# A hybrid decoder trunk on one core: second projection of the first convolution half in one piece, early products along the second half's taps, no ahead splits in short pairs

## Chip, core and metric

The kernel runs on one core of a Trainium2 chip. A core has five engines with their own in-order queues: TensorE (matrix products, PE in the profile, its weight loads PEld), VectorE (DVE), ScalarE (ACT), GpSimd (POOL) and SyncE (SP), which here issues the DMAs. The metric is the device time of one launch in microseconds (us), as the median of several runs.

## What is computed

Two layers over x of 1024 positions by 1024 channels, float32, batch 1:

```
layer 0: x = x + fox_attention(rms_norm(x));   x = x + conv_ffn(rms_norm(x))
layer 1: x = x + conformer_conv(rms_norm(x));  x = x + conv_ffn(rms_norm(x))

conv_ffn(h):        u = causal_dwconv(h @ w_up, w_dw, 3 taps) + b_dw       # w_up: 1024 x 5632
                    gate, val = split(u);  (silu(gate) * val) @ w_down     # w_down: 2816 x 1024
conformer_conv(h):  a, g = split(h @ w_pw1 + b_pw1);  u = a * sigmoid(g)
                    u = silu(rms_norm(causal_dwconv(u, w_dw, 31 taps) + b_dw))
                    u @ w_pw2 + b_pw2                                      # w_pw2: 1024 x 1024
```

Attention, before all this, is not touched by the change.

## The kernel before

Every matrix operand is held as two halves: `hi` is the value rounded to TensorE's faster 4-byte format (a ScalarE cast), `lo` what is left (a subtraction). A product is three passes, hi x hi, hi x lo and lo x hi (`mm3`, lines 183 to 189), into one PSUM bank of 128x512. A "product" in this document is one such pass of 512 columns. Weights come from DRAM raw; `weight` (line 215) casts on ScalarE and lets POOL subtract (`split`, lines 179 to 181), unless a low half lies in DRAM, which is then only loaded. `split_ahead` (line 227) makes such a low half ahead of time: cast on ScalarE, subtraction on VectorE (line 235), two DMAs. The list `T.ahead` holds 76 of them: 32 blocks of the convolution's first projection (`pwlo`), then 44 blocks of layer 0's `w_down` (`dnlo`, 22 row blocks f by two column halves nh).

The tokens are worked in two halves of 512 (h = 0, 1). An up-projection (`up`, line 327) takes the channels in 22 pairs of 128 gate and 128 value channels and computes each pair for both token halves with seven products of 12 passes instead of eight (a Strassen-like scheme): factors t1 to t4 of the activations are made once on VectorE and ScalarE (`combine`, line 258), sums of weights s1 to s4 on POOL. Two of the seven (p1 and p2) need only the first token half, and `early` (line 302) can compute them in advance and park them in DRAM; a pair whose two are parked is a short pair, with five products. In layer 0 nine pairs are short, in layer 1 all 22. Within the loop over pairs (lines 435 to 443) the products p4 and p3 of a pair come after the next pair's first products, and after each pair some ahead splits are recorded:

```
for step in a + before + b:
    step()
before = c
for _ in range(min(ahead[f >= done], len(self.ahead))):   # ahead = (2, 4): short pair 2, full pair 4
    self.ahead.pop(0)()
```

VectorE adds the parked or fresh results (u3 at line 410, u2 at line 400) and does the three taps (line 374) from PSUM, six banks for all.

The down-projection (`down`, line 239) of a token half runs column half by column half; each of its 22 steps f is 12 products into four banks. Its activations are split on VectorE in the first token half of layer 0 and in layer 1, on POOL in the second token half of layer 0 (`los` given). After the second column half the residual x is complete and a norm follows; with `lag` its transposes on TensorE (`norm_block`, line 118) are put off until some products later (`tick`).

The convolution module (`conv`, line 860) also runs by token half, channel tile by channel tile (8). `glu` computes 48 products and u; `taps_of` does 31 taps: 21 on VectorE (line 913), 10 as ScalarE product and POOL addition (lines 905 to 918), then the sum y and, on POOL, the running sum of squares `sqa` (line 927). The norm needs that sum: a row product `ssps` on TensorE (line 944), a broadcast `rb` (line 954), then VectorE and ScalarE make the halves of y (lines 959 to 962). `rest` is the second projection, 192 products in 16 steps, with the late norms behind it.

What order TensorE works in is written by hand, by generators that are advanced in turns (`turns(a, b, n, m)`: n steps of a, then m of b). The other engines' orders are set by a scheduler that plans ahead on the same program; each engine then runs its own queue strictly in that order. The turns around the change, at the end of `trunk`:

- the first convolution half's taps (`main0`) take turns 5 to 2 with the second token half of layer 0's down-projection (`down1`); three more steps of `down1`, then the norm;
- the second half's taps (`main1`) take turns 3 to 1 with a filler: first the second projection of the first half (`rest0`), then the early products of layer 1's up-projection;
- the rest of these early products runs after the second half's projection, beside `combine`.

## Time and profile before

| | |
|---|---|
| runs | 2424.33 us median of 3 (2422.46 to 2425.63) |
| profiled execution | 2430.27 us, span 2428.5 us from first to last instruction |
| TensorE busy | 2281.0 us (94% of the span), mean granted clock 0.972 |
| VectorE busy | 1654.8 us (68%) |
| ScalarE busy | 1410.9 us (58%) |
| POOL busy | 1480.1 us (61%) |
| DMA | 391.88 MB, mean 161 GB/s |

Attention takes about the first 600 us, its output projection to 675, layer 0's up-projection from about 747 to 1158, its down-projection to about 1480, beside it from 1300 the first convolution half; the second half's taps reach to 1731, layer 1's up-projection goes from 1878 to 2180, the last down-projection to the end. Durations come from one execution, and a busy TensorE is not TensorE at its peak, so the waits of TensorE are read from its own rows: the bracket at the end of a row is the idle time in front of it and what ended that.

### The profile page before, as it was taken

Reading aid. Unit: us, or ns where it says so; the run is one execution under the profiler, and the core shown is the slowest. Engines: PE = TensorE matmul, PEld = TensorE weight load, DVE = VectorE, ACT = ScalarE, POOL = GpSimd, SP = SyncE. Lnnn points to the kernel's source line nnn. Section 1 sums busy time; section 2 is a strip of 40 time slices with the busy share of each in tenths; the row PEclk is TensorE's granted clock in tenths of the full one; section 3 lists DMA queues with packets and bytes.
Section 4 is the critical chain, followed back from the end, with each engine's and each line's share of the span. In section 5 each row is a group of like instructions: output and inputs, shape, how many; then the busy total and the mean of one; then the engine's idle time right before and its main releaser. Section 6 shows DMA issues by size and latency. Waiting matters only on the chain. (4 is left out here: it accounts for less than half of the span.)

```text
span 2428.5 us, 35460 instructions
## 1 busy us (share of the span) xinstructions
PE 2281.0 (94%) x11282; PEld 1948.8 (80%) x11282; DVE 1654.8 (68%) x2801; ACT 1410.9 (58%) x2992; POOL 1480.1 (61%) x1258
## 2 busy tenths in 40 slices
PE   7899999999988799998999998978898999999998
PEld 6899999988866678877887886757687888878887
DVE  6577777776384887777645885697427798885554
ACT  6566666665244666666546666566545566664443
POOL 2355554443067767775546887577658999954443
PEclk9999999999989999999999999988899999999999
DMA  4222222252155655556768786463344444566664
GB/s 129 63 78 78 79 79 75 58 199 99 66 172 176 196 170 184 188 190 233 270 201 262 248 272 199 156 195 109 127 152 160 148 152 152 159 210 201 205 214 152
DMA packets 365692, 391.88 MB, mean 161 GB/s; under 512 B 26392, under 2 KB 244288, under 8 KB 365504
## 3 DMA queue, kind: packets, MB, share of 16 engines
q1 hardware_dynamic: 365504, 389.61, 50.4%
q8 instruction: 89, 1.46, 0.2%
q14 instruction: 99, 0.81, 0.1%
HBM read 298.22 MB, written 82.90 MB: 157 GB/s over the span
## 5 line engine op out<-in xcount | busy, mean ns | idle before, releaser
L181 POOL TENSOR_TENSOR wlo<-raw,whi 128x512 fp32r<-128x512 f32 (+1 forms) x368 | 522.1, 1422 | 373.5 <-ACT whi L180 361.7
L180 ACT CAST whi<-raw 128x512 fp32r<-128x512 f32 (+2 forms) x504 | 306.0, 632 | 298.1 <-PE dn L187 191.9
L186 PE MATMUL c<-bhi,whi 128*128 128x512 f32 x880 | 346.4, 394 | 30.8 <-DVE u L410 26.4
L187 PE MATMUL c<-blo,whi 128*128 128x512 f32 x880 | 345.5, 393 | 0.0
L188 PE MATMUL c<-bhi,wlo 128*128 128x512 f32 x880 | 345.0, 392 | 0.0
L374 DVE SCALAR_TENSOR_TENSOR acc<-c,ffntab,acc 128x511 f32<-128x511 f32 (+1 forms) x352 | 280.4, 805 | 89.1 <-ACT edge L367 61.4
L181 DVE TENSOR_TENSOR wlo<-raw,whi 128x512 fp32r<-128x512 f32 (+1 forms) x136 | 182.1, 1342 | 140.1 <-ACT whi L180 139.9
L186 PE MATMUL dn<-whi,whi 128*128 128x512 f32 x704 | 275.4, 391 | 0.0
L187 PE MATMUL dn<-wlo,whi 128*128 128x512 f32 x704 | 274.5, 390 | 0.0
L188 PE MATMUL dn<-whi,wlo 128*128 128x512 f32 x704 | 274.4, 390 | 0.0
L181 POOL TENSOR_TENSOR wlo<-sum,whi 128x512 fp32r<-128x512 f32 x176 | 250.5, 1430 | 29.1 <-ACT whi L180 23.5
L913 DVE SCALAR_TENSOR_TENSOR cacc<-u,ctaps,cacc 128x512 f32<-128x512 f32 x320 | 238.4, 754 | 9.1
L186 PEld LDWEIGHTS c<-bhi,whi 128*128 128x128 f32 x880 | 166.9, 190 | 70.5 <-DVE u L410 20.0
L918 POOL TENSOR_TENSOR pacc<-pacc,prod 128x512 f32<-128x512 f32 x144 | 186.7, 1297 | 22.7 <-ACT prod L917 15.2
L188 PEld LDWEIGHTS c<-bhi,wlo 128*128 128x128 f32 x880 | 167.0, 190 | 35.0
L187 PEld LDWEIGHTS c<-blo,whi 128*128 128x128 f32 x880 | 166.8, 190 | 34.6
L115 POOL TENSOR_SCALAR ss<-ss 128x4 f32<-128x4 f32 (+1 forms) x96 | 21.6, 225 | 272.4 <-ACT hn L123 122.4
L186 PE MATMUL pj<-whi,hthi 128*128 128x384 f32 (+1 forms) x512 | 180.2, 353 | 6.1 <-ACT sqr L583 3.6
L364 ACT ACTIVATE acc<-c,ffntab 128x512 f32<-128x512 f32 x176 | 136.0, 788 | 85.3 <-DMA c<-c11d 53.9
L187 PE MATMUL pj<-wlo,hthi 128*128 128x384 f32 (+1 forms) x512 | 177.9, 347 | 0.6 <-DVE wlo L181 0.6
L188 PE MATMUL pj<-whi,htlo 128*128 128x384 f32 (+1 forms) x512 | 178.1, 348 | 0.0
L671 POOL TENSOR_SCALAR x<-x,nm 128x896 f32<-128x896 f32 (+7 forms) x128 | 100.9, 793 | 106.1 <-DVE nm L670 76.4
(204 smaller groups left out, 5733.8 us busy)
## 6 DMA issues: line engine op xcount, KB each, us to landing
raw<-in_ffn_w_up_dram SPq DMA_DIRECT2D x238, 256.0 KB
raw<-actd SPq DMA_DIRECT2D x176, 256.0 KB
raw<-in_ffn_w_down_dram SPq DMA_DIRECT2D x176, 256.0 KB
raw<-in_conv_w_pw_dram SPq DMA_DIRECT2D x96, 256.0 KB
actd<-acc SPq DMA_DIRECT2D x88, 256.0 KB
wlo<-pwlo SPq DMA_DIRECT2D x64, 256.0 KB
raw<-in_fox_w_in_dram SPq DMA_DIRECT2D x64, 192.0 KB
xd<-x SPq DMA_DIRECT2D x24, 512.0 KB
```

The costliest lines, as they stand in the source:

```text
L115: nc.gpsimd.tensor_scalar(ss, ss, 1.0 / n, EPS, op0=ALU.mult, op1=ALU.add)
L180: self.nc.scalar.copy(hi, raw)
L181: (self.nc.vector if vector else self.nc.gpsimd).tensor_tensor(lo, raw, f32(hi), op=ALU.subtract)
L186: nc.tensor.matmul(out, lh, rh, start=start, stop=False, skip_group_check=more)
L187: nc.tensor.matmul(out, lh, rl, start=False, stop=False, skip_group_check=more)
L188: nc.tensor.matmul(out, ll, rh, start=False, stop=stop, skip_group_check=more)
L364: nc.scalar.activation(acc, ps, AF.Identity, bias=tap[3], scale=tap[2])
L374: nc.vector.scalar_tensor_tensor(acc[:, j:], ps[:, : 512 - j], tap[2 - j], acc[:, j:], op0=ALU.mult, op1=ALU.add)
L671: nc.gpsimd.tensor_scalar(X[:, :L], X[:, :L], nm[:, 2:3], 1.0, op0=ALU.mult, op1=ALU.mult)
L913: nc.vector.scalar_tensor_tensor(acc, win(j), tap(j), acc, op0=ALU.mult, op1=ALU.add)
L918: nc.gpsimd.tensor_tensor(pacc, pacc, t, op=ALU.add)
```

## The change

Four edits. (1) Ahead splits are recorded only after full pairs, four each; none after short pairs, and what is left in the list at the end is not done: 52 of the 76. A `w_down` block without a low half in DRAM is split when it is used. (2) The second projection of the first convolution half runs in one piece before the second half; the second half's taps take turns with early products alone, four to one, once the late norms are through. (3) At the end of both up-projections the down-projection's first two steps are put between the last pair's p7, p4 and p3; x is fetched three steps later. (4) Five instead of three steps of `down1` stand between the first half's taps and its norm.

```diff
--- before
+++ after
@@ -51,7 +51,7 @@
 
 N_POOL = 10
 CONV_DOWN = (5, 2)
-CONV_FILL = (3, 1)
+CONV_FILL = (4, 1)
 LAG = 36
 LEAD = (8, 11)
 
@@ -242,7 +242,7 @@
         pss = [self.pup.tile([P, 512], F32, tag="up", name=self.n("dn")) for _ in range(4)]
         for j, (get, r) in enumerate(zip(lhs, rows)):
             hi, lo = get()
-            wh, wl = self.weight(r[:, m], [P, 512], los[nh][j] if los else None)
+            wh, wl = self.weight(r[:, m], [P, 512], los.get((nh, j)) if los else None)
             for b in range(4):
                 c = slice(b * P, (b + 1) * P)
                 self.mm3(pss[b], hi[:, c], lo[:, c], wh, wl, j == 0, j == len(lhs) - 1)
@@ -324,8 +324,7 @@
                 done.append(g)
                 yield
 
-    def up(self, l, fac, w_up, tab, actd, done, p1d, c11d, ahead):
-
+    def up(self, l, fac, w_up, tab, actd, done, p1d, c11d):
 
         nc = self.nc
         wu = w_up[l].rearrange("(k p) f -> p k f", p=P)
@@ -436,11 +435,12 @@
             for step in a + before + b:
                 step()
             before = c
-            for _ in range(min(ahead[f >= done], len(self.ahead))):
+            for _ in range(min(4, len(self.ahead)) if f >= done else 0):
                 self.ahead.pop(0)()
             yield
         for step in before:
             step()
+            yield
 
     def down_acts(self, xs, l, h, actd, w_down, after, los=None):
 
...
@@ -1077,7 +1078,7 @@
     def early(l, keep):
         yield from T.early(l, keep["ht0"], w_up, keep["p1d"], keep["c11d"], keep["done"], keep["stop"])
 
-    def ffn_up(l, keep, first):
+    def ffn_up(l, keep, first, then):
 
         with ExitStack() as st:
             T.ap = st.enter_context(tc.tile_pool(name=f"act{l}", bufs=1, reuse_waits="tile"))
@@ -1090,13 +1091,18 @@
             turns(T.combine(fac, keep["ht0"], keep["b12"], keep["b22"]), first, 1, (lead + 3) // 4)
             keep["stop"].append(True)
             steps(first)
-            steps(T.up(l, fac, w_up, tabs[l], actd, len(keep["done"]), keep["p1d"], keep["c11d"], (2, 4)))
-            while T.ahead:
-                T.ahead.pop(0)()
+            up = T.up(l, fac, w_up, tabs[l], actd, len(keep["done"]), keep["p1d"], keep["c11d"])
+            steps(up, NF)
+            steps(then, 1)
+            steps(up, 1)
+            steps(then, 1)
+            steps(up)
 
     def ffn_down(l, h, xd, after, los=None):
-        T.fetch_x(xs, xd, h)
-        yield from T.down_acts(xs, l, h, actd, a["ffn_w_down"], after, los)
+        for i, _ in enumerate(T.down_acts(xs, l, h, actd, a["ffn_w_down"], after, los)):
+            if i == 3:
+                T.fetch_x(xs, xd, h)
+            yield
 
     keep = {"xd": xds[0]}
     T.attn_out(a["x"][0], xs, ot, wo, normer(gains[0], keep))
@@ -1115,7 +1121,7 @@
 
     w_pw1 = a["conv_w_pw1"][0]
     pwlo = [[dram.tile([P, 4, P], F32, name=f"pwlo{i}_{q}") for q in range(2)] for i in range(2 * KT)]
-    dnlo = [[dram.tile([P, 512], F32, name=f"dnlo{nh}_{f}") for f in range(NF)] for nh in range(2)]
+    dnlo = {}
     for ct in range(KT):
         for s in range(2):
             for q in range(2):
@@ -1125,9 +1131,15 @@
     for nh in range(2):
         for f in range(NF):
             src = a["ffn_w_down"][0, f * P : (f + 1) * P, nh * 512 : (nh + 1) * 512]
-            T.ahead.append(lambda src=src, lo=dnlo[nh][f]: T.split_ahead(src, lo))
+
+            def make(src=src, i=(nh, f)):
+                dnlo[i] = dram.tile([P, 512], F32, name=f"dnlo{i[0]}_{i[1]}")
+                T.split_ahead(src, dnlo[i])
+
+            T.ahead.append(make)
     begin(0, keep)
-    ffn_up(0, keep, early(0, keep))
+    down0 = ffn_down(0, 0, xds[0], lambda tb: conv_norm(tb))
+    ffn_up(0, keep, early(0, keep), down0)
     keep1 = {"xd": xds[2]}
     begin(1, keep1)
     with ExitStack() as st:
@@ -1149,33 +1161,32 @@
             return T.conv(xs, xds[1], h, hc[h], w_pw1, pwlo, taps, vec, a["conv_w_pw2"][0], halo,
                           normer(gains[2], keep1, True))
 
-        steps(ffn_down(0, 0, xds[0], conv_norm))
+        steps(down0)
         down1 = ffn_down(0, 1, xds[0], conv_norm, dnlo)
         while T.lagging:
             steps(down1, 1)
         main0, norm0, rest0 = conv(0)
         turns(main0, down1, *CONV_DOWN)
-        steps(down1, 3)
+        steps(down1, 5)
         turns(norm0, down1, 1, 1)
         steps(down1)
+        steps(rest0)
+        main1, norm1, rest1 = conv(1)
+
         while T.lagging:
-            steps(rest0, 1)
-        main1, norm1, rest1 = conv(1)
-
-        def fill():
-            yield from rest0
-            while T.lagging:
-                yield
-            yield from early(1, keep1)
-
-        filler = fill()
+            steps(main1, 1)
+        filler = early(1, keep1)
         turns(main1, filler, *CONV_FILL)
         steps(filler, 4)
         turns(norm1, filler, 1, 1)
         steps(rest1)
-    ffn_up(1, keep1, filler)
-    for h in range(2):
-        steps(ffn_down(1, h, xds[2], lambda tb: nc.sync.dma_start(a["out"][0, tb * P : (tb + 1) * P, :], xs[tb])))
+    downs = [
+        ffn_down(1, h, xds[2], lambda tb: nc.sync.dma_start(a["out"][0, tb * P : (tb + 1) * P, :], xs[tb]))
+        for h in range(2)
+    ]
+    ffn_up(1, keep1, filler, downs[0])
+    for g in downs:
+        steps(g)
 
 
 # ---- launch: one core; inputs and outputs as the reference has them ----
```

In the rows of the programs below a name is a tile and its numbers say which buffer.

POOL at the end of the first convolution half, before: `wlo` is a split, `pacc` the addition of a tap, `sqa` the running sum of squares.

```order
L918 TENSOR_TENSOR pacc_16400<-pacc_16400,prod_16474 128x512
L181 TENSOR_TENSOR wlo_16659<-raw_16656,whi_16658 128x512
L918 TENSOR_TENSOR pacc_16400<-pacc_16400,prod_16479 128x512
L181 TENSOR_TENSOR wlo_16701<-raw_16698,whi_16700 128x512
L918 TENSOR_TENSOR pacc_16400<-pacc_16400,prod_16485 128x512
L181 TENSOR_TENSOR wlo_16733<-raw_16730,whi_16732 128x512
L918 TENSOR_TENSOR pacc_16400<-pacc_16400,prod_16490 128x512
L181 TENSOR_TENSOR wlo_16823<-raw_16820,whi_16822 128x512
L918 TENSOR_TENSOR pacc_16400<-pacc_16400,prod_16495 128x512
L927 TENSOR_TENSOR sqa_14719<-sqa_14719,sq_16499 128x512
```

The same place now, from nine rows ahead of the second last sum:

```order
L181 TENSOR_TENSOR wlo_16539<-raw_16536,whi_16538 128x512
L181 TENSOR_TENSOR wlo_16545<-raw_16542,whi_16544 128x512
L181 TENSOR_TENSOR wlo_16655<-raw_16652,whi_16654 128x512
L181 TENSOR_TENSOR wlo_16673<-raw_16670,whi_16672 128x512
L181 TENSOR_TENSOR wlo_16691<-raw_16688,whi_16690 128x512
L919 TENSOR_TENSOR pacc_16001<-pacc_16001,prod_16219 128x512
L181 TENSOR_TENSOR wlo_16735<-raw_16732,whi_16734 128x512
L181 TENSOR_TENSOR wlo_16779<-raw_16776,whi_16778 128x512
L919 TENSOR_TENSOR pacc_16001<-pacc_16001,prod_16224 128x512
L928 TENSOR_TENSOR sqa_14551<-sqa_14551,sq_16228 128x512
L919 TENSOR_TENSOR pacc_16232<-pacc_16232,prod_16237 128x512
L919 TENSOR_TENSOR pacc_16232<-pacc_16232,prod_16242 128x512
```

Before, splits and additions alternate up to the last sum; now the splits come in runs, and all nine additions of the last channel tile stand behind them. Between the sums of channel tiles 3 and 7 there are 22 splits before and 46 now, with 36 additions in both.

TensorE around the broadcast `rb` of the first half's norm, before; `dn` is a bank of a down-projection or of the second projection:

```order
L187 MATMUL dn_15750<-wlo_16665,whi_16658 128x512
L188 MATMUL dn_15750<-whi_16664,wlo_16659 128x512
L954 MATMUL rb_16631<-dg_16680,ones 128x512
L186 MATMUL dn_15747<-whi_16706,whi_16700 128x512
L187 MATMUL dn_15747<-wlo_16707,whi_16700 128x512
```

And now:

```order
L187 MATMUL dn_15582<-wlo_16545,whi_16538 128x512
L188 MATMUL dn_15582<-whi_16544,wlo_16539 128x512
L955 MATMUL rb_16511<-dg_16560,ones 128x512
L186 MATMUL dn_16648<-whi_16654,hthi_3388_16566 128x512
L187 MATMUL dn_16648<-wlo_16655,hthi_3388_16566 128x512
L188 MATMUL dn_16648<-whi_16654,htlo_3390_16568 128x512
```

The 24 products of the down-projection that followed `rb` now stand ahead of the norm's row product, and the second projection, which reads the new halves of y (`hthi`, `htlo`), follows at once.

TensorE at the end of the first up-projection, before (`c` is a bank of the up-projection; the rows go from p7 to p4 of the last pair):

```order
L186 MATMUL c_2587_13038<-bhi_8839,whi_13156 128x512
L187 MATMUL c_2587_13038<-blo_8840,whi_13156 128x512
L188 MATMUL c_2587_13038<-bhi_8839,wlo_13157 128x512
L186 MATMUL c_2587_13038<-bhi_8843,whi_13200 128x512
L187 MATMUL c_2587_13038<-blo_8844,whi_13200 128x512
L188 MATMUL c_2587_13038<-bhi_8843,wlo_13201 128x512
```

And now:

```order
L186 MATMUL c_2551_12902<-bhi_8795,whi_13020 128x512
L187 MATMUL c_2551_12902<-blo_8796,whi_13020 128x512
L188 MATMUL c_2551_12902<-bhi_8795,wlo_13021 128x512
L186 MATMUL dn_13068<-whi_13080,whi_13074 128x512
L187 MATMUL dn_13068<-wlo_13081,whi_13074 128x512
L188 MATMUL dn_13068<-whi_13080,wlo_13075 128x512
```

Twelve products of the down-projection come between p7 and p4, and twelve more between p4 and p3.

## Rows read from the trace of the kernel before

**Rows 1.** Windows by stage: us, busy (count) of PE, PEld, DVE, ACT, POOL, clock, DMA.
```profile
747.00:890.00 143.00, 121.18 (x509) 96.79 (x508) 100.96 (x126) 76.72 (x159) 104.71 (x76) 0.98 0.57 182
...
1144.00:1168.00 24.00, 17.66 (x68) 14.25 (x68) 19.60 (x29) 16.47 (x37) 6.64 (x5) 0.86 1.04 406
...
1615.00:1660.00 45.00, 21.67 (x85) 16.12 (x83) 33.74 (x65) 27.65 (x64) 29.74 (x27) 0.67 0.29 96
...
1850.00:1880.00 30.00, 21.75 (x85) 17.09 (x85) 16.20 (x14) 13.54 (x27) 25.53 (x19) 0.89 0.60 191
1880.00:2170.00 290.00, 290.00 (x1281) 240.15 (x1280) 247.56 (x308) 185.72 (x391) 266.83 (x184) 1.00 0.50 153
2170.00:2195.00 25.00, 22.39 (x93) 18.04 (x92) 20.52 (x28) 15.41 (x32) 7.55 (x6) 0.93 0.86 305
```

**Rows 2.** Timeline of TensorE: start, length, line, tiles [idle before, releaser].
```profile
812.25 0.50 PE L186 MATMUL c<-bhi,whi 128*128 128x512 f32 x1 [3.04 <-DVE u L410]
...
1150.55 0.77 PE L186 MATMUL c<-bhi,whi 128*128 128x512 f32 x1 [6.34 <-DVE u L410]
...
1488.26 1.01 PE L944 MATMUL ssps<-ones,sqa 128*128 128x1 f32 x4 [6.41 <-POOL sqa L927]
...
1731.30 1.86 PE L944 MATMUL ssps<-ones,sqa 128*128 128x1 f32 x8 [9.55 <-POOL sqa L927]
...
1817.64 1.03 PE L132 MATMUL nps<-ident,hn 128*128 128x128 f32 x8
...
1878.62 0.39 PE L186 MATMUL c<-bhi,whi 128*128 128x512 f32 x1
...
2175.14 0.47 PE L186 MATMUL c<-bhi,whi 128*128 128x512 f32 x1 [2.61 <-DVE u L410]
```

**Rows 3.** Window 753 to 890 of line 235 alone: VectorE busy.
```profile
753.00:890.00 137.00, 15.34 (x14) 0.98 0.55 176
```

**Rows 4.** Timeline of VectorE at the end of the first up-projection.
```profile
1143.56 0.69 DVE L235 TENSOR_TENSOR araw<-araw,ahi 128x512 fp32r<-128x512 f32 x1 [1.13 <-ACT ahi L234]
...
1149.72 0.68 DVE L410 TENSOR_TENSOR u<-c,p 128x512 f32<-128x512 f32 x1
```

**Rows 5.** Window 1396 to 1488 of lines 181, 918, 927: POOL busy.
```profile
1396.43:1488.26 91.83, 0.00 (x0) 28.53 (x22) 0.99 0.80 263
1396.43:1488.26 91.83, 46.65 (x36) 0.99 0.80 263
1396.43:1488.26 91.83, 6.46 (x5) 0.99 0.80 263
```

**Rows 6.** Timeline of VectorE around the first half's norm.
```profile
1485.51 0.69 DVE L921 TENSOR_TENSOR y<-cacc,pacc 128x512 f32<-128x512 f32 x1 [9.25 <-POOL pacc L918]
...
1498.16 5.36 DVE L959 SCALAR_TENSOR_TENSOR y<-y,cvec,rb 128x512 f32<-128x512 f32 x8 [5.54 <-PE rb L954]
1503.44 1.24 DVE L962 TENSOR_TENSOR htlo<-y,hthi 128x512 fp32r<-128x512 f32 x1
...
1514.77 1.11 DVE L158 SCALAR_TENSOR_TENSOR htlo<-nps,gtab,hthi 128x128 fp32r<-128x128 f32 x4
```

**Rows 7.** Line 913 (duration ns min/median/max), and VectorE timeline of u.
```profile
L913 DVE SCALAR_TENSOR_TENSOR cacc<-u,ctaps,cacc x320: 743/756/759, 1317.3 to 1720.8; 128x512 f32<-128x512 f32 x160
...
1547.32 0.75 DVE L891 SCALAR_TENSOR_TENSOR u<-pw,cvec,sg 128x512 f32<-128x512 f32 x1 [11.71 <-ACT sg L888]
...
1617.28 0.75 DVE L891 SCALAR_TENSOR_TENSOR u<-pw,cvec,sg 128x512 f32<-128x512 f32 x1 [0.84 <-ACT sg L888]
...
1682.00 0.75 DVE L891 SCALAR_TENSOR_TENSOR u<-pw,cvec,sg 128x512 f32<-128x512 f32 x1 [3.03 <-ACT sg L888]
...
1703.76 0.75 DVE L891 SCALAR_TENSOR_TENSOR u<-pw,cvec,sg 128x512 f32<-128x512 f32 x1 [4.38 <-ACT sg L888]
```

**Rows 8.** Timeline of VectorE, combining of layer 1: first and last operation.
```profile
1819.33 0.85 DVE L278 TENSOR_TENSOR t<-b,hthi 128x512 f32<-128x512 f32 x1
...
1866.96 3.10 DVE L272 TENSOR_TENSOR blo<-t,bhi 128x512 fp32r<-128x512 f32 x5 [2.67 <-ACT bhi L271]
```

More of the change, by code (lines that the diff above doesn't have):

```diff
@@ L858, in conv_tables, with conv @@
         return taps, vec
-    def conv(self, xs, xd, h, ht, w_pw1, los, taps, vec, w_pw2, halo, after, n_pool=N_POOL):
+    def conv(self, xs, xd, h, ht, w_pw1, los, taps, vec, w_pw2, halo, after):
         nc = self.nc
@@ L865, in conv @@
         H = C - 1
+        n_pool = N_POOL
         sp = self.sp
```

## Prediction, before the changed kernel was timed

> **What bounds the kernel.** I read the engine totals first, then the windows by stage, then TensorE's own rows with the wait in front of each, and last the rows of the engine named as releaser. TensorE is busy 94% of the span. From 1880 to 2170 us it runs 1281 matrix products in 290 us, 0.2264 us each, with nothing lost [rows 1]; I use that as the price of one product of 512 columns. TensorE's program holds the same 11141 instructions before and after, so no work is saved there: the change can only move time that TensorE loses. A stretch's loss is its length less its products at 0.2264 us; this includes what the clock costs after a wait (granted clock 0.67 to 0.98 in the windows with losses, 1.00 in the one without).
>
> The stretches that the change touches lose: the short pairs of the first up-projection (747 to 890), 143 - 509 x 0.2264 = 27.8 us; the end of that up-projection (1144 to 1168), 24 - 68 x 0.2264 = 8.6; the end of the second one (2170 to 2195), 25 - 93 x 0.2264 = 3.9; its start (1850 to 1880), 30 - 85 x 0.2264 = 10.8; and the taps of the second convolution half, where 1615 to 1660 alone has TensorE busy 21.7 of 45 us [rows 1]. The waits themselves are in [rows 2].
>
> **A. Short pairs split no weights ahead: -23 us.** A short pair is 60 products, 13.6 us. In the second up-projection all 22 pairs are short and take just that, without ahead splits. In the first, 509 products are 8.5 pairs of 16.9 us, and in seven of the nine pairs the product that needs VectorE's sum u3 (line 410) waits 2 to 3 us, as at 812.25 [rows 2]. The difference between the two is two ahead splits per pair: 14 subtractions at line 235, 15.3 us of VectorE in 137 us [rows 3]. The change takes them out and moves none into the full pairs, which keep four each; 52 splits remain of 76. So these pairs should run as those of layer 1 do: 27.8 us back, less about 5 for the first two pairs, since the second up-projection also loses at its start (1850 to 1880). Bounds: -27.8, and -8 if the wait has another cause.
>
> **B. End of the first up-projection: -7 us.** TensorE waits 6.34 us at 1150.55 for u3 [rows 2]. VectorE is late since, just ahead of it, it does ahead splits which themselves wait for ScalarE (1143.56, 1.13 us; u3 only at 1149.72) [rows 4]; six of them were flushed after the loop. They are gone, and 12 products (2.7 us) of the down-projection now stand in the gap. They need two more subtractions of activations on VectorE (0.7 us each, by the u3 row) and a PSUM bank that is freed just before u3. Of 8.6 us I take back 7; bounds 2 and 8.6.
>
> **C. End of the second up-projection: -2.5 us.** The same 12 products fill a wait of 2.61 us at 2175.14 [rows 2]; bounds 0 and -3.9.
>
> **D. 24 weight splits return to POOL: +18.7 us.** Of the first down-projection's 44 weight blocks only 20 now have a low half in DRAM. The other 24 are split on POOL in its second token half, that is while POOL also adds the first convolution half's taps. Between the squares' sum of channel tile 3 (1396.43) and the row product that ends the norm's wait (1488.26) POOL does 22 splits in 28.53 us, 36 additions in 46.65, 5 sums in 6.46 [rows 5]: 81.6 of 91.8 us, and TensorE at 1488.26 has already waited 6.41 us for the last of these sums [rows 2]. So POOL ends last here, and VectorE with it (9.25 us idle for POOL at 1485.51) [rows 6]. In the changed order 46 splits stand between the same two sums: 24 x 28.53/22 = 31.1 us more. POOL's idle time can take up to 10.5 of it; I let it take 7, since half of the gaps are waits for ScalarE in an order that remains. That is 24.1 us later; but 24 products (5.4 us) that stood behind the norm's row product now stand before it. +18.7. Bounds: +15 with all idle time used, less 5 if ScalarE paces the splits earlier than I think, and +25.7 with none. The DMAs saved (24 low halves written and read) lie beside it and cost nothing now.
>
> The same subtraction took VectorE 0.69 us on its best rows and takes POOL 1.30 [rows 4, 5]. [...]
>
> **E. The first half's norm without cover: +7 us.** Before, 24 products stood between the broadcast of the norm's scale (rb) and the second projection, which needs VectorE's results. Now the second projection follows rb at once. VectorE needs 5.36 us for eight multiplications and 1.24 for the first low half [rows 6]; two wider multiplications come between in the new order, at 0.67 each by the first of these rows. 7.9 us, less rb and the two products that need no low half. Bounds 0 (if the 24 products still cover) and +10.
>
> **F. Second projection in one piece, products ahead along the taps: -3 us.** (1) The projection's 192 products and the first 48 of the next half now run before the first tile u of the taps: 112 products more than before (25.4 us). The old order lost time here: from 1498.16 to the first u at 1547.32 are 49.2 us for 152 products and 32 transposes, some 38 us [rows 6, 7]. About half of the 11 us goes, since products that need no transposed block now stand behind the transposes: first u about 20 us later. (2) From first u to the norm's row product the old order took 1731.30 - 1547.32 = 184.0 us [rows 2, 7]. Its first four channel tiles took 17.5 us each; then the four late norms of the residual stream came between two tiles' taps, and 1617.28 to 1682.00 took 64.7 us for two. In the new order these norms stand in the first tile: VectorE has 21 taps of 0.756, eight groups of four narrow subtractions (1.11 each) and three wider operations (0.75) ahead of the second u [rows 6, 7], 27 us, and TensorE's next 24 products come after the last transposes, so about 37 us. Then the tiles hold 78 products (17.7 us) against VectorE's 21 taps, u and one sum, 17.3: I take 18.3. From last u to the row product 27.5 as before (1703.76 to 1731.30). 37 + 6 x 18.3 + 27.5 = 174.3: 10 us less. (3) Behind it 96 products (21.7 us) fewer remain, all of them from the stretch that hid the combining of the factors (lines 278 to 287). That takes VectorE from 1819.33 to 1870.1 [rows 8]. The last transposes end at 1818.7 and 120 products behind them at 1846; the 24 products that need only the factors made first find work, the ones behind them start at 1870. Before, the up-projection's first product was at 1878.62 and these 24 later, at 1884 [rows 2]: 14 of the 21.7 us are kept. 20 - 10 - 14 = -4; I take -3 for the clock after the new waits. Bounds: -20 and +18.
>
> Sum: -23 - 7 - 2.5 + 18.7 + 7 - 3 = -9.8 us. The profiled execution took 2430.27 us (span 2428.5), so 2420.5 in its frame; the median of the three runs shown, 2424.33, lies 5.9 lower: 2414 us. About 0.2% (5 us) is what a measurement of this kernel can tell from no change.
>
> **Rivals.** R1, the taps of the second half run free: the late norms cost the first tile only 25 us and the rest runs at 17.5, as 1547 to 1617 did. Then F is 12 + 5 lower: 2397 us. For it speaks that pace; against it, that the eight groups are released one by one through two PSUM banks. Chance 0.20.
>
> R2, the other side: with less filler behind them the tiles of the second half are paced by VectorE, POOL and ScalarE together, at 21.8 us as 1682.00 to 1703.76 [rows 7]. 6 x 3.5 = 21 us more, 2435 us, slower. It decides from about 20.8 us per tile on. Against it: that interval held 96 products (21.7 us) and is TensorE's own pace. Chance 0.13.
>
> R3, the short pairs' wait does not come from the splits but from the length of the chain through VectorE or from the reloaded first products: A gives 8 us and not 23: 2429 us. Against it stands the second up-projection, whose pairs have the same chain. Chance 0.10.
>
> My forecast has 0.57, by itself 2403 to 2425. It is faster by over 0.2% in 0.42 of all, within it in 0.12, slower in 0.03; R1 adds 0.20 to faster, R2 0.13 to slower, R3 0.06 to no change and 0.04 to slower. Together 0.62, 0.18, 0.20. The range 2396 to 2434 reaches to the middle of R1 and of R2.
>
> **What would show it.** A: pairs of 13.6 us in the first up-projection, no waits of 3 us for line 409's sum. B, C: at both ends the 12 products inside the gap and under 2 us of wait. D: TensorE waits 20 to 28 us before the first half's row product, with POOL busy all the time; a wait under 12 us refutes it. E: a wait of 6 to 9 us at the second projection's first low half. F: the late norms within the first tile, about 18 us from u to u after that, and a wait of 10 us or more at the second up-projection's first products. The forecast fails if D is absorbed or if the tiles of the second half take over 20 us.

## The result and the profile after

The changed kernel takes 2431.19 us (median of 19 runs, 2426.28 to 2438.66), the kernel before 2424.33 (19 runs beside them): ratio 1.0028, 95% interval 1.0020 to 1.0036. It is slower by some 7 us, where 10 us faster was forecast. Its profiled execution took 2436.2 us (span 2434.4).

The windows of the changed kernel, columns as in [rows 1]:

```profile
748.00:890.00 142.00, 142.00 (x628) 117.56 (x627) 109.75 (x142) 89.37 (x183) 120.68 (x86) 1.00 0.47 148
1116.00:1135.00 19.00, 14.19 (x57) 11.33 (x55) 14.79 (x20) 10.84 (x23) 5.34 (x4) 0.91 0.96 381
...
1872.00:2177.00 305.00, 298.88 (x1297) 246.21 (x1296) 271.71 (x330) 195.30 (x413) 272.59 (x186) 0.98 0.50 154
```

The short pairs (first line) now run 628 products in 142.0 us, 0.226 us each: no loss at all, against 509 in 143 us in [rows 1]. The end of the first up-projection (second line) loses 19 - 57 x 0.2264 = 6.1 us where it lost 8.6. The second up-projection (last line) loses 305 - 1297 x 0.2264 = 11.4 us, nearly all of it at its start: its first 48 products take 22.1 us, where they took 10.9. TensorE's rows at the places of [rows 2], with the waits that are new:

```profile
1123.66 0.77 PE L186 MATMUL dn<-whi,whi 128*128 128x512 f32 x1 [4.81 <-DVE acc L373]
...
1484.14 1.87 PE L945 MATMUL ssps<-ones,sqa 128*128 128x1 f32 x8 [26.63 <-POOL sqa L928]
...
1499.42 0.80 PE L186 MATMUL dn<-whi,hthi 128*128 128x512 f32 x1 [4.06 <-ACT hthi L962]
...
1503.23 0.79 PE L188 MATMUL dn<-whi,htlo 128*128 128x512 f32 x1 [2.60 <-DVE htlo L963]
...
1574.79 1.11 PE L132 MATMUL nps<-ident,hn 128*128 128x128 f32 x4 [7.90 <-DVE htlo L158]
...
1747.96 1.87 PE L945 MATMUL ssps<-ones,sqa 128*128 128x1 f32 x8 [20.61 <-POOL sqa L928]
...
1878.91 0.79 PE L187 MATMUL c<-blo,whi 128*128 128x512 f32 x1 [2.61 <-DVE blo L272]
...
1887.14 0.50 PE L186 MATMUL c<-bhi,whi 128*128 128x512 f32 x1 [2.13 <-DVE u L399]
...
2182.79 0.76 PE L186 MATMUL dn<-whi,whi 128*128 128x512 f32 x1 [3.36 <-DVE acc L373]
```

The two row products of the convolution's norms wait 26.6 and 20.6 us for POOL's running sum, where they waited 6.4 and 9.6 [rows 2]. All other new waits are under 8 us.

Both traces hold the same number of TensorE instructions (11282; the forecast's 11141 stands on neither page of the profile). So the start of one and the same product in both traces tells how far the changed kernel is ahead or behind there. Two such products, before and after (the second product after is in the rows above):

```profile
1301.10 0.49 PE L186 MATMUL pw<-hthi,whi 128*128 128x512 f32 x1 [0.43 <-ACT hthi L155]
...
1503.45 0.39 PE L186 MATMUL dn<-whi,hthi 128*128 128x512 f32 x1
```

```profile
1271.31 0.51 PE L186 MATMUL pw<-hthi,whi 128*128 128x512 f32 x1 [0.44 <-ACT hthi L155]
```

The table is worked out from such rows; the last column is what happened since the line above.

| product or tile | before | after | shift | since then |
|---|---|---|---|---|
| first `c`, layer 0 | 746.99 | 748.41 | +1.4 | +1.4 |
| first `pw` | 1301.10 | 1271.31 | -29.8 | -31.2 |
| first product of the second projection's first half | 1503.45 | 1499.42 | -4.0 | +25.8 |
| first u of the second half | 1547.32 | 1568.51 | +21.2 | +25.2 |
| second half's row product | 1731.30 | 1747.96 | +16.7 | -4.5 |
| 49th `c`, layer 1 | 1889.50 | 1894.35 | +4.9 | -11.8 |
| last product | 2421.42 | 2428.02 | +6.6 | +1.8 |

POOL between the sum of channel tile 3 and the first half's row product, lines 181, 919 and 928 (before: [rows 5]):

```profile
1370.04:1484.14 114.10, 0.00 (x0) 58.36 (x47) 0.90 0.52 165
1370.04:1484.14 114.10, 46.42 (x36) 0.90 0.52 165
1370.04:1484.14 114.10, 6.41 (x5) 0.90 0.52 165
```

46 splits instead of 22 (the view counts one more, which ends just inside the window), the same additions. The three lines add up to 111.2 of 114.1 us, so POOL's idle time, reckoned in this way, fell from 10.2 to 2.9 us, and the stretch is 22.3 us longer. (Neighbouring instructions overlap a little: POOL's own busy time is 80.0 us before and 109.2 now, which gives 11.9 and 4.9 us idle.) VectorE's first, second and last tile u of the second half (before: [rows 7]):

```profile
1568.51 0.75 DVE L892 SCALAR_TENSOR_TENSOR u<-pw,cvec,sg 128x512 f32<-128x512 f32 x1 [9.34 <-ACT sg L889]
...
1603.28 0.75 DVE L892 SCALAR_TENSOR_TENSOR u<-pw,cvec,sg 128x512 f32<-128x512 f32 x1 [5.06 <-ACT sg L889]
...
1709.36 0.75 DVE L892 SCALAR_TENSOR_TENSOR u<-pw,cvec,sg 128x512 f32<-128x512 f32 x1 [0.44 <-ACT sg L889]
```

34.8 us to the second u, 106.1 for the next six (17.7 each on the mean, 19.0 at most), and 38.6 from the last u to the row product. What POOL does in these 38.6 us:

```profile
1726.39 1.29 POOL L919 TENSOR_TENSOR pacc<-pacc,prod 128x512 f32<-128x512 f32 x1
1727.85 1.26 POOL L181 TENSOR_TENSOR wlo<-raw,whi 128x512 fp32r<-128x512 f32 x1 [0.17 <-ACT whi L180]
1729.08 1.26 POOL L919 TENSOR_TENSOR pacc<-pacc,prod 128x512 f32<-128x512 f32 x1
1731.86 1.26 POOL L928 TENSOR_TENSOR sqa<-sqa,sq 128x512 f32<-128x512 f32 x1 [1.53 <-ACT sq L927]
1733.18 11.99 POOL L919 TENSOR_TENSOR pacc<-pacc,prod 128x512 f32<-128x512 f32 x9
1746.64 1.26 POOL L928 TENSOR_TENSOR sqa<-sqa,sq 128x512 f32<-128x512 f32 x1 [1.47 <-ACT sq L927]
```

and VectorE at its end:

```profile
1730.37 0.69 DVE L922 TENSOR_TENSOR y<-cacc,pacc 128x512 f32<-128x512 f32 x1 [1.27 <-POOL pacc L919]
...
1745.21 0.69 DVE L922 TENSOR_TENSOR y<-cacc,pacc 128x512 f32<-128x512 f32 x1 [13.48 <-POOL pacc L919]
```

When the last u is there (1709.36), POOL is still adding for the tile before it, in turn with weight splits of the early products. There is one buffer `pacc`, so the last tile's additions can start only after the y of tile 6 (1730.37); then all nine stand alone, 12 us, and VectorE waits 13.5 us for them. Running TensorE's channel tiles at 17.7 us did not help: from 1625.03 to 1746.64 POOL's sums came every 20.3 us.

### The profile page after: what moved, and what is told of

It is laid out like the page before. It is cut to its first block, busy times and chain, and to the rows that moved or that the text cites. A ratio compares the mean times of both kernels' runs of the same rounds, so it can differ in the third digit from the quotient of the medians.

```text
span 2434.4 us, 35309 instructions
## 1 busy us (share of the span) xinstructions
PE 2275.7 (93%) x11282; PEld 1950.3 (80%) x11282; DVE 1649.0 (68%) x2777; ACT 1398.9 (57%) x2968; POOL 1506.3 (62%) x1282
## 5 line engine op out<-in xcount | busy, mean ns | idle before, releaser
L181 POOL TENSOR_TENSOR wlo<-raw,whi 128x512 fp32r<-128x512 f32 (+1 forms) x392 | 540.6, 1386 | 381.8 <-ACT whi L180 356.7
L180 ACT CAST whi<-raw 128x512 fp32r<-128x512 f32 (+2 forms) x528 | 319.1, 631 | 337.5 <-PE dn L187 202.7
L373 DVE SCALAR_TENSOR_TENSOR acc<-c,ffntab,acc 128x511 f32<-128x511 f32 (+1 forms) x352 | 286.8, 821 | 72.0 <-ACT edge L366 57.3
L181 POOL TENSOR_TENSOR wlo<-sum,whi 128x512 fp32r<-128x512 f32 x176 | 256.6, 1464 | 28.4 <-ACT whi L180 25.0
L919 POOL TENSOR_TENSOR pacc<-pacc,prod 128x512 f32<-128x512 f32 x144 | 186.2, 1293 | 16.9 <-ACT prod L918 9.9
```

Source lines behind the costliest of these rows:

```text
L180: self.nc.scalar.copy(hi, raw)
L181: (self.nc.vector if vector else self.nc.gpsimd).tensor_tensor(lo, raw, f32(hi), op=ALU.subtract)
L373: nc.vector.scalar_tensor_tensor(acc[:, j:], ps[:, : 512 - j], tap[2 - j], acc[:, j:], op0=ALU.mult, op1=ALU.add)
L919: nc.gpsimd.tensor_tensor(pacc, pacc, t, op=ALU.add)
```

## Experiments

Theory S is that the two POOL queues (D before the first norm, and the last tile of F) and the lost cover cost what the short pairs gain, each by itself. Ratios are to the kernel before, on the same chip.

**1. Splits alone.** The kernel before with edit 1 only (`ahead` (0, 4), nothing flushed; `dnlo` is filled as in the change). In this and the other diffs, `...` marks lines left out.

```diff
...
-            steps(T.up(l, fac, w_up, tabs[l], actd, len(keep["done"]), keep["p1d"], keep["c11d"], (2, 4)))
-            while T.ahead:
-                T.ahead.pop(0)()
+            steps(T.up(l, fac, w_up, tabs[l], actd, len(keep["done"]), keep["p1d"], keep["c11d"], (0, 4)))
...
```

> The kernel before with edit (1) alone: no ahead splits after short pairs, four after full pairs, the 24 blocks left over are split on POOL when they are used. Theory S (the change is the sum of a gain of 28 us in the short pairs and of losses made elsewhere, the largest of them by the 24 splits on POOL): short pairs 28 us shorter; POOL ends 25 us later in the first convolution half, where TensorE waits about 31 us before the norm's row product (26.8 in the changed kernel, whose 24 products stand ahead of it); in all -28 + 25 and a little for the flush that is gone, 2416 to 2422 us. Rival Q (the wait of 27 us comes from the new place of the five steps and the order around the norm, not from the splits): wait near the 6.4 us of before, 2396 to 2400 us.

Measured: 2418.87 us, 0.9989 (0.9980 to 0.9998). The row product of the first half:

```profile
1481.61 1.87 PE L944 MATMUL ssps<-ones,sqa 128*128 128x1 f32 x8 [27.51 <-POOL sqa L927]
```

From 748 to 890 us it runs 628 products, as the changed kernel does, and its row product waits 27.5 us. The short pairs' gain and POOL's loss are both there and nearly cancel. So edits 2 to 4 are what makes the whole change slower than before.

**2. Six splits in full pairs.** The changed kernel, all 76 splits made.

```diff
-            for _ in range(min(4, len(self.ahead)) if f >= done else 0):
+            for _ in range(min(6, len(self.ahead)) if f >= done else 0):
```

> The changed kernel, but six ahead splits after each full pair instead of four, so that all 76 blocks have a low half and none of the 24 is split on POOL. Theory S: the wait before the first half's row product falls from 26.8 to about 1 us (6.4 less the 24 products ahead of it), 20 us less; the full pairs, 19 us of TensorE each, carry two more subtractions of 0.7 us on VectorE and may lose 0 to 8 us over 13 pairs: 2411 to 2420 us. Rival Q: wait stays above 20 us, 2431 us or more.

Measured: 2451.26 us, 1.0128 (1.0110 to 1.0145). TensorE, full pairs and the first half's row product:

```profile
911.81 0.79 PE L186 MATMUL c<-hthi,whi 128*128 128x512 f32 x1 [3.99 <-ACT p L389]
...
1501.67 1.05 PE L945 MATMUL ssps<-ones,sqa 128*128 128x1 f32 x8 [2.02 <-POOL sqa L928]
```

The wait for POOL is gone, as S says of its cause, but the full pairs cannot carry six: from 890 to 1110 us they run 798 products where the changed kernel runs 956, that is 158 x 0.2264 = 36 us. The windows of the changed kernel and of this one:

```profile
890.00:1110.00 220.00, 217.82 (x956) 178.71 (x955) 160.42 (x214) 142.91 (x294) 165.76 (x124) 1.00 0.60 188
```

```profile
890.00:1110.00 220.00, 194.44 (x798) 156.96 (x797) 150.12 (x201) 123.42 (x259) 141.82 (x101) 0.94 0.64 205
```

The price expected for them, 0 to 8 us, was wrong. In the traces the stretch from the first `c` to the first `pw` is 43 us longer than in the changed kernel, and 27 of these come back on the way to the second projection.

**3. The 24 blocks on VectorE.** `weight` gets a flag, which it hands on to `halves`; it puts the subtraction on VectorE for the `w_down` blocks without a low half.

```diff
...
-            return self.halves(raw, shape)
+            return self.halves(raw, shape, vector)
...
-            wh, wl = self.weight(r[:, m], [P, 512], los.get((nh, j)) if los else None)
+            wh, wl = self.weight(r[:, m], [P, 512], los.get((nh, j)) if los else None, bool(los))
```

> The changed kernel, but the 24 blocks without a low half are subtracted on VectorE and not on POOL when they are used. Theory S: POOL has 31 us less to do between the sums of channel tiles 3 and 7, VectorE 24 x 0.69 = 17 us more beside 70 of 92 us; the wait of 26.8 us falls below 8 us: 2410 to 2416 us. Rival Q: the wait stays above 20 us, about 2431 us. If VectorE takes POOL's place as the bound, the wait falls to 10 to 20 us only.

Measured: 2414.51 us, 0.9974 (0.9964 to 0.9984).

```profile
1467.23 1.87 PE L945 MATMUL ssps<-ones,sqa 128*128 128x1 f32 x8 [10.53 <-POOL sqa L928]
```

The row product comes 16.9 us earlier than in the changed kernel and the total falls by 0.54% (13 us): D is POOL's queue. The wait left, 10.5 us, is longer than S expected (under 8), and VectorE has not become the bound instead: at 1463.55 it waits 6.05 us for POOL's last addition. Between the sum of channel tile 3 and the row product, 13 of POOL's 26 splits take 1.71 to 1.78 us and the others 1.26 to 1.30, some 6 us in all (see the last section).

**4. The projection as filler.** The changed kernel with edit 2 undone (three to one, `rest0` ahead of the early products in the filler).

```diff
-CONV_FILL = (4, 1)
+CONV_FILL = (3, 1)
...
-        steps(rest0)
+        while T.lagging:
+            steps(rest0, 1)
...
```

> The changed kernel with edit (2) undone: the second projection is again filler of the second half's taps, three to one, with early products after it. Theory S (this edit lost 9 us: 25 us later first u, and a wait of 21 us before the second half's row product in place of 10): the wait is 9 to 10 us again, the late norms stand between two tiles again, 2420 to 2424 us. Rival F+ (products ahead along the taps pay, and the 9 us come from what is late behind the first half's norm): 2431 us or more, since 96 products go back under the combining, where they cover less.

Measured: 2417.87 us, 0.9986 (0.9977 to 0.9995); the second half's row product waits 9.57 us, as S says; the time is a little below the range expected. Edit 2 costs about 10 us, and with it undone the rest of the change is a small gain.

**5. Both.** Experiments 3 and 4 together.

> The changed kernel with two of its costs taken out at once: the 24 down-projection blocks without a low half are subtracted on VectorE, and the second projection is the filler of the second half's taps again (three to one). Theory S (the two costs are separate: about 14 us by POOL's splits before the first half's norm, about 10 us by the order behind it): the gains add up, 2404 us in the frame of the 2421 us of the kernel before, 0.993 of it; TensorE waits about 10 us at the first half's row product and about 10 us at the second's. Rival T (both edits take away the same lag of POOL, so one is enough): 2412 to 2415 us, 0.997.

Measured: 2402.34 us, 0.9921 (0.9903 to 0.9938). The gains add up (0.54% + 0.42% off 1.0028 gives 0.9932); T falls.

**6. Three steps.** The same with edit 4 undone.

```diff
-        steps(down1, 5)
+        steps(down1, 3)
```

> As the kernel with both costs taken out, but with three instead of five steps of the second token half's down-projection between the first half's taps and its norm, as before the change: the 24 products stand behind the broadcast rb again and cover the norm, and no longer stand ahead of its row product. Theory S (what the 24 products cover on one side they uncover on the other): the wait at the first half's row product is 5 us longer, the one at the second projection's first low half 6 us shorter or gone, and the time is within 3 us of the kernel with five steps. Rival (the 5.4 us in front of the row product are hidden by POOL anyway, the 7 us behind rb are not): 5 to 7 us faster.

Measured: 2401.89 us, 0.9914 (0.9898 to 0.9931). The wait at the row product grows from 10.5 to 12.6 us, the waits behind `rb` (4.10 and 2.45 us in experiment 5) shrink to 0.68, and another of 3.9 us stands at the late norms' transposes. Edit 4 moves the loss from one side of the norm to the other, as S says. The times alone do not exclude the rival's 5 us, since the intervals overlap; the traces do, with 252.2 us from the first `pw` to the first u of the second half against 253.2 in experiment 5.

**7. The last tile.** The changed kernel; the second half's last channel tile gives POOL 5 taps instead of 10.

```diff
-        n_pool = N_POOL
...
+            n_pool = 5 if h == 1 and ct == KT - 1 else N_POOL
...
```

> The changed kernel, in whose second convolution half the last channel tile gives 5 taps instead of 10 to ScalarE and POOL and 26 instead of 21 to VectorE. Theory S (the second half's row product comes 38.6 us after the last u because POOL, late by the early products' weight splits, does nine additions of the last tile alone at its end, 1.33 us each): four additions are left, so the wait of 20.8 us at that row product shrinks by 5 to 7 us, and the time by 4 to 7: 0.9998 to 1.0010 of the kernel before. Rival T (VectorE's taps or TensorE's own pace set the end): VectorE's five more taps make it 3 to 4 us later, 1.0045.

Measured: 2422.31 us, 1.0001 (0.9990 to 1.0013), 0.27% (6.5 us) better than the changed kernel. POOL and TensorE:

```profile
1730.48 5.30 POOL L919 TENSOR_TENSOR pacc<-pacc,prod 128x512 f32<-128x512 f32 x4
```

```profile
1738.56 1.87 PE L945 MATMUL ssps<-ones,sqa 128*128 128x1 f32 x8 [13.91 <-POOL sqa L928]
```

Four additions instead of nine, the wait 6.7 us shorter, the whole of it in the total: the additions of the last tile set the end.

**8. Three to one.** The changed kernel with `CONV_FILL = (3, 1)`, the projection still in one piece.

> The changed kernel with the second half's taps three to one with early products instead of four to one; the second projection still runs in one piece. More of the early products stand between two channel tiles. Theory S (POOL sets the pace of the sums, about 20.3 us per channel tile, and TensorE's products run ahead of it): u to u goes from 17.7 to about 20 to 21 us, the stretch from last u to the row product falls by 8 to 12 us, the row product itself moves by no more than 5 us, and what the tiles take more of products is missing behind the norm; total within 4 us of the changed kernel. Rival T (each additional early product brings its own splits to POOL, so the sums fall further behind): the row product comes 10 us or more later and the time is 5 to 10 us longer.

Measured: 2425.5 us, 1.0012 (1.0003 to 1.0021). From the last u (1719.80) to the row product it is 30.8 us instead of 38.6, but the last u is 10.4 us later and the row product 2.7:

```profile
1750.61 1.87 PE L945 MATMUL ssps<-ones,sqa 128*128 128x1 f32 x8 [10.11 <-POOL sqa L928]
```

Reckoned from the first u, the row product comes 5.6 us later (185.0 us for 179.4), and POOL's sums come every 21.6 us instead of 20.3. So the products added, with their splits, cost POOL something, but less than rival T said: TensorE does 72 products more (16.3 us) before that row product, most of them in what was its wait. The time falls by 0.16%, near the 4 us that S allowed.

**9. Eight taps in the last tile.** Experiment 6 with `n_pool = 8` in the second half's last tile.

> The kernel with both costs taken out and three steps, in whose second convolution half the last channel tile gives 8 taps instead of 10 to ScalarE and POOL. Theory S (VectorE waits 6.9 us for POOL's last addition there, and TensorE 9.7 us for what follows): two additions of 1.3 us fewer on POOL, two taps of 0.75 more on VectorE, which has the room: the wait at the row product is 7 us and the time 2 to 3 us lower, about 2399 in the frame of 2422 us of the kernel before, 0.9905. Rival (ScalarE's products set the end of POOL's row of additions): no change.

Measured: 2396.96 us, 0.9902 (0.9887 to 0.9916), the fastest of all. The row product:

```profile
1702.81 1.87 PE L945 MATMUL ssps<-ones,sqa 128*128 128x1 f32 x8 [6.87 <-POOL sqa L928]
```

The trace is as expected; the gain of 0.12% over experiment 6 is within the two intervals.

**10. The ends as before.** Experiment 6 with edit 3 undone.

> The kernel with both costs taken out and three steps, with the ends of both up-projections as they were before the change (edit 3 undone). Theory S (the first down-projection's banks are freed no sooner than the sum that TensorE waited for, so most of the wait only moves): the end of the first up-projection waits 8.4 us where it waits 4.0, the end of the second 1.5 where it waits 3.1; total 2 to 4 us longer. Rival P (as forecast, terms B and C): 9 us longer, 0.9952 of the kernel before. Rival N (other units of the banks): no change at all.

Measured: 2405.28 us, 0.9935 (0.9921 to 0.9948), 0.21% above experiment 6, with overlapping intervals: between S and P, nearer to S; the times alone would also allow N (no change). The end of the first up-projection, without and with edit 3:

```profile
1121.42 0.77 PE L186 MATMUL c<-bhi,whi 128*128 128x512 f32 x1 [8.55 <-DVE u L409]
```

```profile
1120.83 0.76 PE L186 MATMUL dn<-whi,whi 128*128 128x512 f32 x1 [3.79 <-DVE acc L373]
```

The wait shrinks by 4.8 us and has another releaser. From the first `c` to the first `pw` the trace with edit 3 is 3.6 us shorter. At the second end the wait is 1.73 us without the edit (2150.54) and 2.95 with it (2152.22).

**11. Two in short pairs.** The changed kernel, short pairs make two splits again (70 of 76).

```diff
-            for _ in range(min(4, len(self.ahead)) if f >= done else 0):
+            for _ in range(min(4 if f >= done else 2, len(self.ahead))):
```

> The changed kernel, but each of the nine short pairs of the first up-projection makes two ahead splits again, so that 70 of the 76 are made and 6 down-projection blocks are left without. Theory S (term A and term D of the forecast are both real, and the change trades one for the other): the short pairs lose about 25 to 28 us again, as before the change; the wait of 26.8 us at the first half's row product falls to 10 to 13; nothing moves behind it; 10 to 13 us longer than the changed kernel, 1.0075 of the kernel before. Rival R3 (the short pairs' wait has another cause): the pairs stay at 13.6 us, and with 15 us gained at the row product the time is 0.997 of the kernel before.

Measured: 2446.43 us, 1.0098 (1.0084 to 1.0112). The window of the short pairs, and the first half's row product:

```profile
748.00:890.00 142.00, 130.16 (x532) 104.04 (x531) 104.86 (x133) 81.12 (x169) 105.89 (x75) 0.94 0.57 182
```

```profile
1493.17 1.87 PE L945 MATMUL ssps<-ones,sqa 128*128 128x1 f32 x8 [12.81 <-POOL sqa L928]
```

96 products fewer in the window (21.7 us) and 13.8 us less wait at the row product. The time is 0.70% (17 us) above the changed kernel where 10 to 13 us were expected; the two traces are 11 us apart. Both terms are real, and the short pairs' wait comes from the splits; R3 falls.

## Why the prediction was wrong

| term | forecast | measured in the trace |
|---|---|---|
| A, short pairs | -23 | -27.8 |
| B, end of the first up-projection | -7 | -3.4 |
| D and E, POOL's splits and the norm without cover | +25.7 | +25.8 |
| F (1), to the first u | +20 | +25.2 |
| F (2), first u to the row product | -10 | -4.5 |
| F (3), behind the row product | -14 | -11.8 |
| C, end of the second up-projection | -2.5 | +1.8 |
| start of layer 0 | 0 | +1.4 |

**The step that failed** is in F (2): "From last u to the row product 27.5 as before". It took 38.6 us. The steps beside it came out a little better than forecast (34.8 us for 37, 17.7 per tile for 18.3), so the 11.1 us are what is wrong there. I took the stretch from the old order, where POOL's sums of tiles 5, 6 and 7 began 25.2, 26.3 and 26.2 us after their u, and gave the new tiles the pace of TensorE and VectorE alone; now these sums begin 33.4, 38.8 and 37.3 us after u. POOL was counted in D but not in F. Its splits by channel tile, from sum to sum in the changed kernel (window, length, busy, count, clock, DMA):

```profile
1644.79:1663.82 19.03, 3.92 (x4) 1.00 0.63 194
1663.82:1682.67 18.85, 2.65 (x3) 1.00 0.63 195
1682.67:1707.35 24.68, 10.36 (x8) 1.00 0.68 228
1707.35:1731.86 24.51, 10.37 (x9) 0.98 0.54 179
```

In tiles 5 and 6 the splits rise to 8 each, from 3 and 2 in the tiles before (the view's counts take in one that reaches over an edge). POOL is busy 22.9 of 24.7 and 22.6 of 24.5 us there, the sums take 24.6 us each where u comes every 17.7, and the last nine additions stand uncovered. Experiment 7 gives back 6.5 us by taking five of them away, experiment 4 about 10 by the old order. No run takes the splits of tiles 5 and 6 away; that they delay the sums is read from these rows. R1 falls with the first tile's 34.8 us (it had 25). Rival R2 named the right engine among its three, but not the mechanism: u to u stayed at 17.7 us on the mean, below the 20.8 from which it was to decide; only POOL's sums ran at 20.3.

**B and C were mis-sized.** VectorE at the end of the first up-projection of the changed kernel:

```profile
1120.33 0.68 DVE L409 TENSOR_TENSOR u<-c,p 128x512 f32<-128x512 f32 x1
...
1122.78 0.73 DVE L373 SCALAR_TENSOR_TENSOR acc<-c,ffntab,acc 128x510 f32<-128x510 f32 x1
```

Nine of the 12 products fill the gap; the tenth needs the fourth bank, and the tap (line 373) that lets it go ends at 1123.5, 2.5 us behind the sum that was waited for before. I took that bank to be freed just before u3, and it is the other way round. So waits of 4.81 and 3.36 us stand at the two ends, where under 2 were forecast. At the second end, where the wait was only 2.6 us [rows 2], nothing is gained. The 1.8 us lost there lie within what the traces scatter: from the 49th `c` to the last product it is 529.6 to 534.1 us in those with edit 3 and 529.1 to 531.9 in the three without.

**A was right in mechanism** and larger than forecast: I kept 5 us for the first two pairs, which lost nothing. Experiment 11 shows the cause.

**D and E** were right in mechanism: the 24 splits take 29.8 us (forecast 31.1), POOL's idle time took 7.3 of them (7), the wait is 26.6 us (20 to 28), and behind `rb` 4.06 and 2.60 us are lost (6 to 9). That their sum is met within 0.1 us is luck. The first half's row product is 25.7 us later against the first `pw`, which is 20.2 without its 24 products (D: 18.7); 3.4 us of this were lost before the stretch that was reckoned with. From the row product to the second projection 5.5 us are lost (E: 7). Experiment 3 shows D's cause, experiment 6 that E and the 24 products of D are one trade.

**F (1)** is 5 us too low: half of the old loss was to go, and none went. From the second projection's first product to the first u 240 products stand where 132 stood, 24.5 us more, and the loss (the transposes included) is 69.1 - 54.3 = 14.8 us where it was 43.9 - 29.9 = 14.0. The waits for the late norms' transposes did shrink, from 1.03 and 3.90 us to 1.47 and 0.24. But the low half is now waited for 2.60 us instead of 0.66, and the products around that wait run at a granted clock of 0.50 instead of 1.00. The windows behind the first products, before and now:

```profile
1503.45:1510.00 6.55, 5.89 (x25) 4.33 (x24) 6.02 (x10) 6.55 (x14) 0.97 (x3) 1.00 0.81 267
```

```profile
1503.23:1508.00 4.77, 4.77 (x11) 3.79 (x12) 4.17 (x7) 2.99 (x7) 4.77 (x1) 0.50 0.12 51
```

The larger wait of 7.90 us at 1574.79 stands behind the first u, in the 34.8 us of the first tile.

**F (3)**: 2 us less were kept. The single wait of 10 us that was forecast did not come; the factors' last halves come late in parts (1.37 us at 1875.79, 2.61 at 1878.91, 2.13 at 1887.14), and the products between run in part at a granted clock of 0.50 (from 1878.91 to 1882 and from 1888 to 1890).

In the traces forecast and result differ by 16.4 us: F 12, C 4, B 4, the start 1, less 5 in A. (F was put at -3 in all, with 1 us for the clock that has no line in the table.) Less the 11.1 us of the step that failed, all else the same, the changed kernel would have ended 4.5 us ahead. What stays open is which part of F (1) belongs to the clock and which to the low half's wait; no run separates them.

## What to carry to other kernels

Where work is moved to an engine that is "free" on average, count its queue over each stretch that ends in a wait, the last tile above all: what an in-order queue still holds when its last input comes is the wait (here nine additions, 12.0 us), and a single accumulator buffer forbids starting it earlier. A stretch's length may be taken over from the old order only if the queues of all engines at its start are the same. An edit that fills a wait with other products needs their buffers free before the wait ends, or the wait only changes its name (here 4.81 us).

## What was not expected of the hardware

A short wait can cost more than itself. After the 4.81 us at 1123.66 the next products start 0.43 us apart until 1126.78, nearly twice the 0.2264 of a steady stretch; the granted clock is 0.50 there. After the 26.6 us at 1484.14 this lasts until 1491.99, at 0.50 too. The 3.04 us at 812.25 in the kernel before [rows 2] cost only themselves: the clock stayed at 1.00. The changed kernel, then the kernel before:

```profile
1123.66:1126.78 3.12, 3.12 (x7) 2.48 (x8) 1.41 (x2) 1.71 (x3) 1.14 (x1) 0.50 1.05 421
```

```profile
812.25:815.00 2.75, 2.75 (x12) 2.29 (x13) 1.86 (x3) 0.94 (x3) 1.31 (x1) 1.00 1.02 317
```

VectorE's and POOL's subtractions can take longer side by side than alone. In the changed kernel VectorE's takes 0.68 us at 1121.58, where POOL is idle, and 1.77 us at 1110.76, beside one of POOL's that began at 1110.25 and takes 1.74. VectorE and POOL in experiment 3:

```profile
1447.82 0.81 DVE L181 TENSOR_TENSOR wlo<-raw,whi 128x512 fp32r<-128x512 f32 x1
1448.56 1.54 DVE L914 SCALAR_TENSOR_TENSOR cacc<-u,ctaps,cacc 128x512 f32<-128x512 f32 x2
1450.00 1.60 DVE L181 TENSOR_TENSOR wlo<-raw,whi 128x512 fp32r<-128x512 f32 x1
```

```profile
1448.02 1.78 POOL L181 TENSOR_TENSOR wlo<-raw,whi 128x512 fp32r<-128x512 f32 x1
1449.75 1.29 POOL L919 TENSOR_TENSOR pacc<-pacc,prod 128x512 f32<-128x512 f32 x1
1451.00 1.76 POOL L181 TENSOR_TENSOR wlo<-raw,whi 128x512 fp32r<-128x512 f32 x1
```

The 24 splits take 0.68 to 1.75 us on VectorE, and those of POOL up to 1.78 (1.28 to 1.34 at the same place in the changed kernel), while the taps, which accumulate in PSUM, keep 0.74 to 0.76. Why the splits lengthen and the taps do not, no run shows.
